# Output weights of the second pair: the first cast, low part and first sum later in their attention period

## The chip, the core and the metric

The kernel runs on one core of a Trainium2 chip. The core has five engines with instruction queues of their own: TensorE (PE, matrix products), VectorE (DVE), ScalarE (ACT), GpSimd (POOL) and SyncE (SP, which here issues the transfers between the chip's memory, HBM, and the core's own memory). Each engine takes its instructions in the order in which they stand; a wait at the head of a queue holds up everything behind it. The metric is the device time of one execution in microseconds (us).

## The reference

The kernel computes one encoder block on 512 tokens of width 2048 in float32:

```
h  = RMSNorm(x)
[qa|ka|va|qb|kb|vb|f] = h @ W_in
oa = stick-breaking attention (8 heads)      ob = forgetting attention (8 heads)
x  = x + concat(headnorm(oa), headnorm(ob)) @ W_out
x  = x + relu(RMSNorm(x) @ W_up)^2 @ W_down
y  = RMSNorm(x)
```

The change concerns `W_out`, 2048 x 2048, while the attention runs: its rows are prepared there for the product that comes behind the attention.

## The kernel before, in words

Every float32 product is made of three products of parts. An operand is split into a high part, a copy rounded to float32r (ACT, "cast"), and a low part, the difference (DVE, "low"); `mm3` (L76 to L79) multiplies high by high, low by high and high by low.

The attention stage handles 16 heads in 17 periods of a written timetable, `TPER` = 26.05 units each. In period n, PE projects the query and the key of head n, forms the scores of head n - 1 and the value product and the norm's sums of head n - 2, all in turn. The projections use four weight pieces per period (`Piece`, load L163 on SP into `wraw`, cast L170 on ACT into `wh`, low part L177 on DVE into `wl`), two for the query and two for the key.

For a head of the forgetting kind, DVE adds the biases to the scores (L840), GpSimd masks them (L779), DVE takes row maxima (L847, L848), ACT the exponentials (L852), and DVE divides by the row sums (L855, L857). ACT then sets the 16-bit halves apart (L872), SP transposes them in a transfer (L876), ACT joins them again (L880) and splits them (L884, with L887 on DVE). After the value product (tile `o`), ACT squares it, copies it and casts the square (L928, L929, L930); DVE makes the square's low part (L933); PE sums over the partitions with two matmuls (L938, L939, tile `ssq`); ACT and DVE finish the norm (L942, L943, L948 to L951). The query's result is scaled (L739), cast (L743, tile `uh`) and its low part made (L747, tile `ul`): these are "the query's parts". The key's are made by the same lines, with L737 ahead, at the beginning of the next period.

Beside this the output weights are prepared, in pairs of rows by `WeightSums`. For the pairs m = 0 to 3 (`whole`) a pair takes two periods, of which the first starts at `e` and the second at `o` = `e` + `TPER`. Two transfers (L968) bring four blocks into the tile `mixed`, which is free until the heads' results go there. The first cast (L972, `high`) and low part (L975, `low`) go to the tile `tboth`, which is stored to `wraws` (L976); four sums (L980, `sum`), a sixth cast and low part (L984, L988) follow, and stores (L989, L992).

The order of all this is a table: `plan.at(t, f)` enters a step at a time t, `plan.run` sorts by t and issues the steps so. The times are no waits; they only set the order on PE, ACT and DVE. The loads and stores on SP follow the table too up to entry 55.05; behind it a scheduler places them by its own estimates, between what they depend on. For m = 1, `e` is the start of period 2 in the table (52.1).

Of the kernel before, what the change touches and what calls it, by code (L numbers as in the profile page):

```python
# [37 lines left out]
def block_kernel(ctx, tc, x, g_attn, w_in, b_f, g_out_sb, g_out_fox, w_out, g_mlp, w_up, w_down, g_final, y):  # L38
# [104 lines left out]
    def v_columns(h):  # L143
        return 2 * WSB + h * P if h < NH else o0 + 2 * WSB + (h - NH) * P
# [74 lines left out]
    with ExitStack() as stage:  # L219
# [70 lines left out]
        c0, m = v_columns(order[0]), 2 * P + NH  # L290
# [422 lines left out]
    with tc.tile_pool(name="att", bufs=1, side="right", reuse_waits="tile") as at, \  # L713
# [281 lines left out]
        def whole(m, t):  # L995
            w = WeightSums(m, (0, 1), lambda: mixed[:, :NH].rearrange("p (q a) n -> p q (a n)", a=2))
            e, o = (t, t + TPER) if m else (TPER, TPER)
            loads = (0.5 if m == 1 else -15.0, 2.7) if m else (20.5, 20.6)
            highs, lows_, sums_, sixth = ((e + 3.3, o + 3.3), (e + 4.5, o + 4.5), (e + 6.4, e + 16.3, o + 6.4, o + 16.3), (o + 10.7, o + 20.6)) if m > 1 else \
                ((e + 10.7, o + 3.3), (e + 11.15, o + 4.5), (e + 16.3, e + 24.9, o + 6.4, o + 16.3), (o + 10.7, o + 20.6)) if m else \  # L1000
                ((e + 4.0, e + 10.0), (e + 5.2, e + 11.0), (e + 6.4, e + 19.2, e + 20.6, e + 21.8), (e + 22.0, e + 24.0))
            for i in range(2):
                plan.at(t + loads[i], w.load, (i,))
                plan.at(highs[i], w.high, i)
                plan.at(lows_[i], w.low, i)
            for i in range(4):
                plan.at(sums_[i], w.sum, i)
            plan.at(sums_[1] + 0.1, lambda: w.store(0, 2))
            plan.at(sixth[0], w.high_6)
            plan.at(sixth[1], w.low_6)  # L1010
            plan.at(sixth[1] + 0.1, lambda: w.store(2, 4))
# [132 lines left out]
        for m in range(4):  # L1144
            whole(m, TPER * 2 * m)
# [764 lines left out]
    def down_at(k):  # L1910
        g, db, i, p, u0 = down[k]
        return g, db, i, p, u0, min(2, GROUPS[g][1] - u0)

    with tc.manual_schedule(engines={pe.engine, act.engine, dve.engine}):
        for k in range(-4, len(down)):
            g, db, i, p, u0, m = down_at(max(k, 0))
# [198 lines left out]
```

## Time and profile before

| | us |
|---|---|
| median of 3 runs | 2012.35 |
| their range | 2009.54 to 2012.75 |
| the profiled execution | 2012.1 |
| its span in the profile | 2010.4 |
| busy PE, DVE, ACT in the span | 1997.9, 1738.8, 1202.2 |

The profile shows one execution. Rows of a timeline give the start, the duration, the engine, the line in the kernel, the operation, the tile written and the tiles read, and in brackets how long the engine was idle before it and what ended this. In a row of matmuls, which overlap, the duration is longer than the step from one start to the next. Rows of the waits give the total, the count and the longest. Rows of windows give, for each stretch, its length, the busy time and count of PE, of PE's weight loads, DVE, ACT and POOL, the clock granted to PE (1.00 is full), the busy share of the transfer engines and GB/s. The attention stage lies at about 150 to 620 us of the span; the periods' boundaries are not marked in the trace, but the scores' matmuls (tile `s`) and the norm's sums (tile `ssq`) show which one it is. What stands at about 200 to 226 us is period 2, with query and key of head 2, softmax of head 1 and norm of head 0.

### The profile page before, as it was taken

How to read it: one execution, taken by the hardware profiler on the slowest of the kernel's cores; microseconds unless marked ns; L12 is line 12 of the kernel's file. 1: busy time of each engine (PE TensorE's matmuls, PEld its weight loads, DVE VectorE, ACT ScalarE, POOL GpSimd, SP SyncE). 2: the span in 40 equal slices, each digit the busy share in tenths (PEclk: the TensorE clock that was granted, in tenths of full speed). 3: DMA queues.
4: the chain of work that ended last, by engine and by line, in shares of the span. 5: the costliest groups of instructions: out<-in, count | busy, mean ns of one | idle time of the engine just before them, and what ended most of it. 6: DMA issues, size and time to landing. Idle time of an engine off the chain costs nothing.

```text
span 2010.4 us, 27058 instructions
## 1 busy us (share of the span) xinstructions
PE 1997.9 (99%) x10302; PEld 1730.5 (86%) x10302; DVE 1738.8 (86%) x1968; ACT 1202.2 (60%) x1645; POOL 58.3 (3%) x73
## 2 busy tenths in 40 slices
PE   9999999999999999999999999999999999999998
PEld 9998788888898889888888888888888888888887
DVE  7886777788878578999999999998798888988896
ACT  7544666777765565777676766767543444444344
POOL 0000000011110000000000000000000000000003
PEclk9999999999999999999999999999999999999999
DMA  7417877777668872566666676666794674674642
GB/s 253 161 68 247 269 241 215 212 212 217 207 218 279 292 255 95 172 208 209 207 190 211 194 222 189 210 199 235 252 327 172 232 273 153 234 264 170 216 161 86
DMA packets 309426, 423.54 MB, mean 211 GB/s; under 512 B 49408, under 2 KB 205104, under 8 KB 302768
## 3 DMA queue, kind: packets, MB, share of 16 engines
q1 hardware_dynamic: 308544, 419.71, 63.8%
q10 hardware_dynamic: 752, 2.11, 0.3%
q8 instruction: 81, 1.33, 0.3%
q14 instruction: 49, 0.40, 0.1%
HBM read 315.45 MB, written 96.49 MB: 205 GB/s over the span
## 4 chain that ended last, share of the span: by engine, by line
PE 96%; DVE 1%; DMA 1%; ACT 0%; SPq 0%; issue 0%; ACTq 0%; DVEq 0%
PE psa L1287 11%; PE accd L78 8%; PE accd L79 8%; PE accd L77 8%; PE psa L1285 6%; PE psc L1287 5%; PE accq L77 5%; PE accq L79 5%; PE accq L78 5%; PE psc L1285 3%; PE psb L1287 3%; PE psb L1285 1%; PE m L78 1%; PE m L77 1%; PE m L79 1%; PE accoa L79 1%
## 5 line engine op out<-in xcount | busy, mean ns | idle before, releaser
L1923 ACT CAST wh<-wd 128x1024 fp32r<-128x1024 f32 x126 | 124.9, 999 | 168.7 <-PE accd L79 61.0
L1809 DVE TENSOR_TENSOR wl<-wu,wh 128x1024 fp32r<-128x1024 f32 x158 | 192.8, 1220 | 12.1 <-ACT wh L1803 11.9
L77 PE MATMUL accq<-hH,wh 128*128 128x512 f32 x512 | 200.8, 392 | 0.0
L79 PE MATMUL accq<-hH,wl 128*128 128x512 f32 x512 | 200.1, 391 | 0.0
L78 PE MATMUL accq<-hL,wh 128*128 128x512 f32 x512 | 199.8, 390 | 0.0
L1803 ACT CAST wh<-wu 128x1024 fp32r<-128x1024 f32 x158 | 167.5, 1060 | 43.8 <-issue 26.7
L1287 PE MATMUL psa<-f,wh 128*128 128x512 f32 x720 | 179.0, 391 | 0.0
L78 PE MATMUL accd<-wl,uf 128*128 128x512 f32 x436 | 169.6, 389 | 0.0
L79 PE MATMUL accd<-wh,uf 128*128 128x512 f32 x436 | 169.6, 389 | 0.0
L77 PE MATMUL accd<-wh,uf 128*128 128x512 f32 x436 | 169.4, 389 | 0.0
L1287 PEld LDWEIGHTS psa<-f,wh 128*128 128x128 f32 x720 | 132.3, 188 | 25.6
L1930 DVE TENSOR_TENSOR wl<-wd,wh 128x1024 fp32r<-128x1024 f32 x126 | 144.1, 1152 | 10.6 <-ACT wh L1923 10.6
L1923 ACT CAST wx<-wd 128x1024 fp32r<-128x1024 f32 (+1 forms) x82 | 80.8, 994 | 106.9 <-PE accd L79 43.4
L1644 DVE TENSOR_TENSOR m<-m,accd 128x1024 f32<-128x1024 f32 x84 | 102.3, 1218 | 47.1 <-PE accd L79 47.1
L79 PEld LDWEIGHTS accq<-hH,wl 128*128 128x128 f32 x512 | 96.4, 188 | 20.4
L78 PEld LDWEIGHTS accq<-hL,wh 128*128 128x128 f32 x512 | 96.6, 189 | 19.3
L77 PEld LDWEIGHTS accq<-hH,wh 128*128 128x128 f32 x512 | 96.6, 189 | 19.0
L77 PE MATMUL accd<-wx,uf 128*128 128x512 f32 x284 | 110.5, 389 | 0.0
L78 PE MATMUL accd<-wx,uf 128*128 128x512 f32 x284 | 110.5, 389 | 0.0
L79 PE MATMUL accd<-wx,uf 128*128 128x512 f32 x284 | 110.5, 389 | 0.0
L1285 PEld LDWEIGHTS psa<-f,wl 128*128 128x128 f32 x720 | 96.0, 191 | 5.4
L1285 PE MATMUL psa<-f,wl 128*128 128x256 f32 x720 | 98.3, 282 | 0.0
(443 smaller groups left out, 5118.1 us busy)
## 6 DMA issues: line engine op xcount, KB each, us to landing
wu<-in_w_up_dram SPq DMA_DIRECT2D x60, 1024.0 KB, 6.5
ufd<-st SPq DMA_DIRECT2D x98, 512.0 KB, 3.9
wd<-in_w_down_dram SPq DMA_DIRECT2D x48, 1024.0 KB, 8.5
uf<-ufd SPq DMA_DIRECT2D x42, 1024.0 KB, 7.5
wraw<-in_w_in_dram SPq DMA_DIRECT2D x68, 512.0 KB, 6.0
wo<-wsums SPq DMA_DIRECT2D x28, 512.0 KB, 4.4
q<-in_w_in_dram SPq DMA_DIRECT2D x32, 384.0 KB, 5.6
wd<-in_w_down_dram SPq DMA_DIRECT2D x16, 768.0 KB, 5.4
```

Of the source, the lines that this page charges most:

```text
L77: pe.matmul(out, sh, mh, start=first, stop=False, skip_group_check=True)
L78: pe.matmul(out, sh, ml, start=False, stop=False, skip_group_check=True)
L79: return pe.matmul(out, sl, mh, start=False, stop=last, skip_group_check=True)
L1285: ins = pe.matmul(ps[:, 2 * P:], lo[:, a, :], f_parts(p, a)[0], start=False, stop=last, skip_group_check=True)
L1287: ins = pe.matmul(ps, hi[:, a, :], f_both(p, a), start=a == PAIRS[0] and p in (1, 5), stop=last, skip_group_check=True)
L1644: dve.tensor_tensor(M[p][:, :, db, :], M[p][:, :, db, :], ps, op=ALU.add)
L1803: act.copy(rooms[k][0], srcs[k])
L1809: lows[0] = dve.tensor_tensor(lo, srcs.pop(k), hi.bitcast(F32), op=ALU.subtract)
L1923: act.copy(rooms[k + 3][0], srcs[k + 3])
L1930: dve.tensor_tensor(rooms[k + 2][1], srcs.pop(k + 2), rooms[k + 2][0].bitcast(F32), op=ALU.subtract)
```

## The change

The table's entries of the pair m = 1 change in three places; the middle branch of the three is that of m = 1.

```
             highs, lows_, sums_, sixth = ((e + 3.3, o + 3.3), ...) if m > 1 else \
-                ((e + 10.7, o + 3.3), (e + 11.15, o + 4.5), (e + 16.3, e + 24.9, o + 6.4, o + 16.3), (o + 10.7, o + 20.6)) if m else \
+                ((e + 19.0, o + 3.3), (e + 20.55, o + 4.5), (e + 20.6, e + 24.9, o + 6.4, o + 16.3), (o + 10.7, o + 20.6)) if m else \
```

The first cast moves from `e` + 10.7 to `e` + 19.0, the first low part from `e` + 11.15 to `e` + 20.55, the first sum from `e` + 16.3 to `e` + 20.6. PE's and GpSimd's orders stay as they are; the number of instructions does too.

On ACT, in period 2, these rows stood before, from the cast of the third weight piece on (`tboth` holds the high and low part of the output weights, `pl` here is the square's high part):

```order
L170 CAST wh<-wraw 128x1024
L972 CAST tboth<-mixed 128x512
L170 CAST wh<-wraw 128x1024
L852 ACTIVATE w,ml<-w,ml 128x128
L852 ACTIVATE w,ml<-w,ml 128x256
L852 ACTIVATE w,ml<-w,ml 128x384
L852 ACTIVATE w,ml<-w,ml 128x512
L928 ACTIVATE ph<-o 128x512
L929 COPY os<-o 128x512
L930 CAST pl<-ph 128x512
L743 CAST uh<-qf 128x512
L942 ACTIVATE ra<-ssq,eps 128x512
```

And these stand there now:

```order
L170 CAST wh<-wraw 128x1024 x2
L852 ACTIVATE w,ml<-w,ml 128x128
L852 ACTIVATE w,ml<-w,ml 128x256
L852 ACTIVATE w,ml<-w,ml 128x384
L852 ACTIVATE w,ml<-w,ml 128x512
L928 ACTIVATE ph<-o 128x512
L929 COPY os<-o 128x512
L930 CAST pl<-ph 128x512
L743 CAST uh<-qf 128x512
L972 CAST tboth<-mixed 128x512
L942 ACTIVATE ra<-ssq,eps 128x512
```

The cast L972 left the place between the third and the fourth piece's casts and stands behind the query's cast L743, ahead of the norm's L942.

On DVE, at the same place of the program, before (L887 is the low part of head 0's transposed weights, the L177 rows are the third and the fourth piece's low parts):

```order
L887 TENSOR_TENSOR pl<-pt,ph 128x1280
L975 TENSOR_TENSOR tboth<-mixed,tboth 128x512
L177 TENSOR_TENSOR wl<-wraw,wh 128x1024
L847 TENSOR_REDUCE ml<-w 128x1 x4
L848 TENSOR_SCALAR ml<-ml 128x4
L739 SCALAR_TENSOR_TENSOR qf<-accq,rb 128x512
L177 TENSOR_TENSOR wl<-wraw,wh 128x1024
L980 TENSOR_TENSOR mixed<-mixed 128x1024
L855 RECIPROCAL ml<-ml 128x4
```

And now, from the fourth piece's low part on; ahead of it the rows are the same without L975:

```order
L177 TENSOR_TENSOR wl<-wraw,wh 128x1024
L855 RECIPROCAL ml<-ml 128x4
L857 TENSOR_SCALAR w<-w,ml 128x128
L857 TENSOR_SCALAR w<-w,ml 128x256
L857 TENSOR_SCALAR w<-w,ml 128x384
L857 TENSOR_SCALAR w<-w,ml 128x512
L933 TENSOR_TENSOR pl<-ph,pl 128x512
L747 TENSOR_TENSOR ul<-qf,uh 128x512
L975 TENSOR_TENSOR tboth<-mixed,tboth 128x512
L980 TENSOR_TENSOR mixed<-mixed 128x1024
L948 SCALAR_TENSOR_TENSOR ph<-ssq,ra 128x512
```

L975 and L980 left their places ahead of the row maxima and ahead of the reciprocal; both stand behind the query's low part L747 and ahead of the norm's L948.

On SP, the store of `tboth` (L976) and the load of the next period's first weight piece (L163) change places:

```order
 L968 DMA mixed<-in_w_out_dram 128x2048
-L976 DMA wraws_93<-tboth 128x2x512
-L163 DMA wraw<-in_w_in_dram 128x8x128
+L163 DMA wraw<-in_w_in_dram 128x8x128
+L976 DMA wraws_93<-tboth 128x2x512
 L876 DMA_TRANSPOSE pl<-pt 128x20x128
```

The store now stands directly ahead of the transposing transfer of head 1.

## The prediction

> **What bounds the kernel now.** I read the page's busy times first, then the waits of TensorE, then the clock around the longest wait, and last the engines' timelines there.
>
> ```profile
> PE 1997.9 (99%) x10302; PEld 1730.5 (86%) x10302; DVE 1738.8 (86%) x1968; ACT 1202.2 (60%) x1645; POOL 58.3 (3%) x73
> ```
> ```profile
> PE ssq L938 <- ACT pl L930: 2.5, 1, 2.5
> PE vx L303 <- DVE still L299: 1.6, 1, 1.6
> PE ssq L939 <- DVE pl L933: 0.5, 1, 0.5
> ```
>
> TensorE (PE) is busy for 99% of the span, so only time that PE loses counts. Its waits are few: one at the start (L303), and the two matmuls of one sum of squares, L938 and L939, which head 0's norm needs in period 2 (n = 2, about 200 to 226 us). All other periods have none. The same place is the only stretch inside the kernel's attention stage where the granted clock (PEclk, the column behind POOL) drops:
>
> ```profile
> 221.00:222.00 1.00, 0.14 (x1) 0.00 (x0) 1.00 (x2) 1.00 (x5) 0.00 (x0) 1.00 0.99 389
> 224.00:225.00 1.00, 0.50 (x2) 0.41 (x2) 1.00 (x2) 0.06 (x1) 0.00 (x0) 0.82 0.19 58
> 225.00:226.00 1.00, 1.00 (x3) 0.74 (x3) 0.14 (x1) 0.59 (x1) 0.00 (x0) 0.50 0.00 0
> 228.00:229.00 1.00, 1.00 (x5) 0.81 (x5) 0.93 (x3) 0.98 (x1) 0.00 (x0) 0.98 0.00 0
> ```
> ```profile
> 220.52 0.39 PE L78 MATMUL accq<-hL,wh 128*128 128x512 f32 x1
> 220.75 0.39 PE L79 MATMUL accq<-hH,wl 128*128 128x512 f32 x1
> 223.59 0.50 PE L938 MATMUL ssq<-pl,onesr 128*128 128x512 f32 x1 [2.45 <-ACT pl L930]
> 224.59 0.78 PE L939 MATMUL ssq<-pl,onesr 128*128 128x512 f32 x1 [0.50 <-DVE pl L933]
> 225.17 0.63 PE L77 MATMUL accq<-hH,wh 128*128 128x512 f32 x1
> 228.12 0.40 PE L78 MATMUL accq<-hL,wh 128*128 128x512 f32 x1
> ```
>
> In step with the matmuls ahead of it, which start every 0.23 us (220.52, 220.75), L938 would have started at 220.98. It starts at 223.59, L939 a whole microsecond later, and the eight matmuls up to 228.12 run at half clock for the most part. From 220.98 to 228.12 stand 10 steps (two of the sum, eight of the projection, the last beginning at 228.12): at full rate 9 x 0.23 = 2.07 us for the nine that precede it, against 7.14 us. This place costs 5.1 us, and that is the most that the change can win here.
>
> Who is late is seen on ScalarE (ACT) and VectorE (DVE):
>
> ```profile
> 215.42 0.62 ACT L972 CAST tboth<-mixed 128x512 fp32r<-128x512 f32 x1 [3.42 <-DMA mixed<-in_w_out_dram]
> 216.94 1.05 ACT L170 CAST wh<-wraw 128x1024 fp32r<-128x1024 f32 x1 [0.90 <-DMA wraw<-in_w_in_dram]
> 219.77 0.40 ACT L852 ACTIVATE w<-w,ml 128x128 f32<-128x128 f32 x1 [1.78 <-DVE ml L848]
> 222.91 0.62 ACT L930 CAST pl<-ph 128x512 fp32r<-128x512 f32 x1
> 223.43 0.62 ACT L743 CAST uh<-qf 128x512 fp32r<-128x512 f32 x1
> 225.41 0.69 ACT L942 ACTIVATE ra<-ssq,eps 128x512 f32<-128x512 f32 x1 [1.36 <-PE ssq L939]
> 226.67 2.31 ACT L872 COPY pt<-w 128x2560 uint16<-128x2560 uint16 x1
> ```
> ```profile
> 211.09 1.49 DVE L887 TENSOR_TENSOR pl<-pt,ph 128x1280 fp32r<-128x1280 f32 x1 [0.84 <-ACT ph L884]
> 216.07 0.69 DVE L975 TENSOR_TENSOR tboth<-mixed,tboth 128x512 fp32r<-128x512 f32 x1 [3.49 <-ACT tboth L972]
> 216.68 1.22 DVE L177 TENSOR_TENSOR wl<-wraw,wh 128x1024 fp32r<-128x1024 f32 x1
> 217.82 1.66 DVE L847 TENSOR_REDUCE ml<-w 128x1 f32<-128x128 f32 x4
> 219.51 0.17 DVE L848 TENSOR_SCALAR ml<-ml 128x4 f32<-128x4 f32 x1
> 220.19 1.21 DVE L177 TENSOR_TENSOR wl<-wraw,wh 128x1024 fp32r<-128x1024 f32 x1
> 221.32 1.22 DVE L980 TENSOR_TENSOR mixed<-mixed 128x1024 f32<-128x1024 f32 x1
> 222.66 1.27 DVE L857 TENSOR_SCALAR w<-w,ml 128x128 f32<-128x128 f32 x4
> 223.85 0.69 DVE L933 TENSOR_TENSOR pl<-ph,pl 128x512 fp32r<-128x512 f32 x1
> ```
> ```profile
> 206.40 8.94 DMA mixed<-in_w_out_dram
> ```
>
> The load of the output weights' first half (mixed) lands at 215.34. ACT's cast L972 waits 3.42 us for it, DVE's L975 waits 3.49 us for the cast. Behind L975 stand, in order, a weight piece's low part (L177), head 1's row maxima (L847, L848), and only then may ACT begin the exponentials (L852). Behind these stand L928, L929 and L930, for which L938 waits. So a load that nobody needs here soon holds up the chain L975, L177, L847, L848, L852, L930, L938.
>
> **The change, part by part.** Three compute instructions move, nothing is added: the cast (0.62 us, row 215.42), the low part (0.69, row 216.07) and the sum (1.22, row 221.32), and with the low part its store (wraws), which falls behind a load on SP's queue.
>
> *ACT without L972.* The next instruction is L170, the cast of the period's fourth piece. It waited for its own load until 216.94, after L972 had left, and that load does not hang on the moved work; it is issued ahead of it on SP:
>
> ```profile
> 206.95 4.94 SPq L163 DMA_DIRECT2D wraw<-in_w_in_dram  x2
> 216.79 0.38 SPq L976 DMA_DIRECT2D wraws<-tboth  x1
> 217.93 0.49 SPq L163 DMA_DIRECT2D wraw<-in_w_in_dram  x1
> 229.00 2.52 SPq L876 DMA_TRANSPOSE pl<-pt  x1
> ```
>
> The row at 206.95 merges two piece loads, the second of which is the fourth piece's. I keep 216.94: ACT is then free at 217.99 (1.05 us). Its next start overlaps the end by 0.10, as row 222.91 with its 0.62 us and row 223.43 show.
>
> *DVE without L975.* L887 ends at 212.58, so L177 can run from 212.5 to 213.7, the four maxima (1.66) to 215.4 and L848 to 215.5. That is before ACT is free. So L852 starts at 217.89, where the cast lets it, and not at 219.77: 1.88 us earlier. L930 keeps its distance, ends at 221.65 (before 222.91 + 0.62 = 223.53), and L938 starts at 221.71. PE's wait falls from 2.45 to about 0.6 us.
>
> *DVE without L980.* L933, for which L939 waits, stood behind L177, L980 and L857. L177 of the fourth piece now follows its cast (218.05 to 219.27); the reciprocal needs the last exponential (about 220.2), L857 ends near 221.7, and L933 runs from 221.70 to 222.39. L939 starts at 222.44, 2.15 us earlier than 224.59. The gap that L980 leaves is filled by the wait for ACT, so of its 1.22 us only what lies in these 2.15 is won.
>
> *The clock.* The gap in PE shrinks from 2.45 + 0.50 us to about 0.6 + 0.4. No row shows what a gap of one microsecond does to the clock. Bounds: the slow stretch stays as it is (gain 2.15 alone), or goes. If it goes, the projection's first matmul starts 0.35 us behind L939 (0.58 at half clock in the rows 224.59 and 225.17, less 0.23 by which a full-rate step is shorter), and seven more at 0.23 bring the matmul of 228.12 to 224.40: gain 3.72 us. I take this: by the windows' means the half clock lasted from about 224.64 (0.82 is 0.36 us at half) to 228.04 (0.98), if the two microseconds between are like 225 to 226. These 3.4 us stand just behind 3.4 us in which PE did almost nothing but L938, while in the new order it idles for 1.0 us of them and works for over two thirds.
>
> [...]
>
> *Where the moved work now stands.* On ACT L972 comes behind L743 and ahead of L942, which waits for L939. L743 ends at about 222.2, L972 at 222.7, L942 cannot start before 223.1: hidden by that wait (ACT stood idle 1.36 us at row 225.41). On DVE L975 and L980 run from 222.9 to 224.7, where L948 waits for L943 until about 224.4: some 0.3 us later than it could be, and off PE's path. On SP the store is issued at about 223.7; the transposing load (row 229.00), which waits for L872 to end at about 226.7, is behind it. The queue's one other passed item, the next piece's load of 217.93, waits for the L177 that ended at 217.90 and now ends at 213.7; it can only go out earlier.
>
> *Is the gain kept?* PE is 3.72 us ahead in period 3, while the store and the transposes are only about 2.1 us ahead. In that period head 1's sum has these rows:
>
> ```profile
> 242.79 0.62 ACT L984 CAST thi<-mixed 128x512 fp32r<-128x512 f32 x1 [1.54 <-DMA wraws<-tboth]
> 249.23 0.62 ACT L930 CAST pl<-ph 128x512 fp32r<-128x512 f32 x1
> ```
> ```profile
> 250.17 0.68 DVE L933 TENSOR_TENSOR pl<-ph,pl 128x512 fp32r<-128x512 f32 x1
> ```
> ```profile
> 252.21 0.39 PE L938 MATMUL ssq<-pl,onesr 128*128 128x512 f32 x1
> 252.44 0.39 PE L939 MATMUL ssq<-pl,onesr 128*128 128x512 f32 x1
> ```
>
> L930 ends 2.36 us and L933 1.6 us before PE takes them. The difference of 3.72 - 2.15 = 1.6 us between PE's lead and the transfers' lead uses up this slack and does not pass it. I cost it at nothing, with L984's wait for the second store (1.54 us now) as what is late next.
>
> Sum: the profiled execution took 2012.1 us, 1.7 more than its span; 2012.1 - 3.72 = 2008.4 us. The median shown, 2012.35, is 0.25 above this execution, so against it the gain is 0.20%, and 0.2% (4.0 us, about what a measurement of this kernel can tell from no change) lies at 2008.33.
>
> **The rivals.**
>
> One, *the stall goes whole*: if the fourth piece lands 0.6 us earlier than 216.94, L938 is in step and PE wins the 5.1 us: 2007.0. For it speaks that this landing ends a backlog of transfers and that the runs lie 3.2 us apart (2009.54 to 2012.75); against it, that nothing in the change speeds that load.
>
> Two, *the gap shrinks and the slow clock stays* (the slow stretch has another cause than this gap), or the fourth piece lands late: 2012.1 - 2.15 = 2010.0. Each microsecond by which the piece lands past 216.94 takes one off the gain, and past 218.8 nothing of the earlier L852 is left. Against it: PE's idle time falls to a third.
>
> Three, *slower*: period 3's store of the second tboth decides. L984 waits for its landing already, and L763, L170, L852 and L930 stand behind it on ACT. It lands at 242.79 now. If transfers are the limit there it moves up 2.1 us, to 240.7, and L933 ends just in time. From there on PE waits a microsecond for each. With the slow clock that a wait of 2.45 us brings (1.6 us, the difference of 3.72 and 2.15) the gain is gone at a landing of 242.8, and one at 246.8 gives about 2012.1 - 3.7 + 6.1 + 1.6 = 2016.1. For it: transfers are dense in this stage. Against it: the moved store goes out where the transfers stand idle (PE rows 225 to 229 have DMA share 0.00), so less is queued, not more.
>
> A fourth, small: part of this happens and the new wait gives back some 2 us: 2010.5.
>
> **How the numbers follow.** The sum's own case gets 0.54, with its own range 2007.3 to 2009.5 (0.5 us either way for the piece's landing, 0.3 for the steps between, and the 0.25 between profiled and median run); half of it lies below 2008.33. Rival one gets 0.22, rival two 0.11, the fourth 0.06, rival three 0.07. Faster by over 0.2%: 0.22 + 0.27 = 0.49; slower: 0.07; the rest, 0.44, within 0.2%. The range 2006.8 to 2010.8 holds the sum's case, most of rival one and two and part of the fourth, and leaves out rival three and the tails.
>
> **What would show it.** In the changed profile L972 stands behind L743 with no wait ahead of it. L170 ahead of L852 still waits for its load, now for nearly 5 us, and ends near 218. L938 waits about 0.6 us for L930, L939 a few tenths for L933, and PEclk is 1.00 from 221 to 229. L948 follows L980 without a gap. In period 3 no PE wait appears. The prediction is wrong if PEclk still drops, if the fourth piece lands at another time, or if PE's list of waits has a new row after 230 us.

## The result, and the profile after

The changed kernel takes 2007.91 us (median of 16 runs, 2006.98 to 2011.13), the kernel before 2011.77 (16 runs, 2008.33 to 2012.99). The ratio is 0.9983, with an interval of 0.9976 to 0.9990. So 3.9 us are gained, 0.17%, clear of the measurement's noise and just within the 0.2% named in the prediction. The profiled execution took 2007.39 us. Of all executions reported below, one, of the kernel with ten extra matmuls, took 2848.28 us at a mean clock of 0.654; it is a slow one and is left out of every count and median here.

TensorE's waits and the granted clock (the third figure from the end in each row of the windows) after the change:

```profile
PE vx L303 <- DVE still L299: 1.6, 1, 1.6
PE ssq L938 <- ACT pl L930: 0.3, 1, 0.3
PE accoa L79 <- DVE g L60: 0.3, 1, 0.3
PE ssq L939 <- DVE pl L933: 0.2, 1, 0.2
```
```profile
224.00:225.00 1.00, 1.00 (x6) 0.84 (x5) 0.97 (x2) 1.00 (x1) 0.00 (x0) 1.00 0.91 350
225.00:226.00 1.00, 1.00 (x6) 0.81 (x5) 0.93 (x3) 0.60 (x1) 0.00 (x0) 1.00 0.00 0
```

The waits for L930 and L933 fell from 2.45 and 0.50 us to 0.31 and 0.23, and the clock stays at 1.00. The order of the queues is the one forecast, seen in the timelines of ACT, DVE and SP:

```profile
216.00 1.05 ACT L170 CAST wh<-wraw 128x1024 fp32r<-128x1024 f32 x1 [4.88 <-DMA wraw<-in_w_in_dram]
216.96 0.39 ACT L852 ACTIVATE w<-w,ml 128x128 f32<-128x128 f32 x1
220.09 0.62 ACT L930 CAST pl<-ph 128x512 fp32r<-128x512 f32 x1
221.13 0.62 ACT L972 CAST tboth<-mixed 128x512 fp32r<-128x512 f32 x1
222.03 0.69 ACT L942 ACTIVATE ra<-ssq,eps 128x512 f32<-128x512 f32 x1 [0.28 <-PE ssq L939]
```
```profile
212.75 1.66 DVE L847 TENSOR_REDUCE ml<-w 128x1 f32<-128x128 f32 x4
220.75 0.69 DVE L933 TENSOR_TENSOR pl<-ph,pl 128x512 fp32r<-128x512 f32 x1
221.96 0.69 DVE L975 TENSOR_TENSOR tboth<-mixed,tboth 128x512 fp32r<-128x512 f32 x1
222.68 1.22 DVE L980 TENSOR_TENSOR mixed<-mixed 128x1024 f32<-128x1024 f32 x1
223.82 0.68 DVE L948 SCALAR_TENSOR_TENSOR ph<-ssq,ra 128x512 f32<-128x512 f32 x1
```
```profile
214.98 0.38 SPq L163 DMA_DIRECT2D wraw<-in_w_in_dram  x1
222.67 0.38 SPq L976 DMA_DIRECT2D wraws<-tboth  x1
225.62 2.52 SPq L876 DMA_TRANSPOSE pl<-pt  x1
```

The maxima (L847) run at 212.75 instead of 217.82. ACT now waits 4.88 us for a weight piece's load, and the exponentials (L852) follow it without a gap. L972, L975 and L980 stand where nothing of the chain is behind them, and L948 follows L980 at once. On PE the place reads:

```profile
220.07 0.39 PE L79 MATMUL accq<-hH,wl 128*128 128x512 f32 x1
220.77 0.49 PE L938 MATMUL ssq<-pl,onesr 128*128 128x512 f32 x1 [0.31 <-ACT pl L930]
221.49 0.50 PE L939 MATMUL ssq<-pl,onesr 128*128 128x512 f32 x1 [0.23 <-DVE pl L933]
221.83 0.39 PE L77 MATMUL accq<-hH,wh 128*128 128x512 f32 x1
223.44 0.39 PE L78 MATMUL accq<-hL,wh 128*128 128x512 f32 x1
```

In step, L938 would have started at 220.30; the eighth matmul of the projection starts at 223.44. That is 3.14 us for what took 7.14 before, 4.0 us less. Of these, 2.4 lie ahead of L939 (1.19 us from the step to L939's start, 3.61 before) and 1.6 behind it (1.95 against 3.53): wait and clock. The two profiled spans differ by 4.7 us (2010.4 and 2005.7). The other 0.7 us were there before the place: the last matmul ahead of L938 starts at 220.07 here and at 220.75 there, and the transfer L755, ahead of every instruction that moved, is issued at 195.03 here and at 195.75 there. They belong to the two executions, not to the change.

### The profile page after: what moved, and what is told of

The parts are those of the page before. It is cut to its first block, busy times and chain, and to the rows that moved or that the text cites. A ratio compares the mean times of both kernels' runs of the same rounds, so it can differ in the third digit from the quotient of the medians.

```text
span 2005.7 us, 27059 instructions
## 1 busy us (share of the span) xinstructions
PE 1995.6 (99%) x10302; PEld 1729.5 (86%) x10302; DVE 1738.9 (87%) x1968; ACT 1202.1 (60%) x1645; POOL 58.0 (3%) x73
## 4 chain that ended last, share of the span: by engine, by line
PE 97%; DMA 1%; DVE 1%; ACT 0%; issue 0%; SPq 0%; ACTq 0%; DVEq 0%
PE psa L1287 11%; PE accd L78 8%; PE accd L79 8%; PE accd L77 8%; PE psa L1285 6%; PE psc L1287 5%; PE accq L77 5%; PE accq L79 5%; PE accq L78 5%; PE psc L1285 3%; PE psb L1287 3%; PE psb L1285 1%; PE m L77 1%; PE m L79 1%; PE m L78 1%; PE accoa L79 1%
```

## The experiments

The theory: the low part L975 stood at the head of DVE's queue, waiting by way of L972 for a load, and held up the maxima and so the exponentials, the norm's cast and PE; PE's idle time then made the clock fall. The rivals: the sum on DVE or the cast on ACT did it; the weight piece's load did it; the clock's fall has another cause.

**The sum alone.** Cast and low part stay.

```
-                (..., (e + 16.3, e + 24.9, o + 6.4, o + 16.3), ...) if m else \
+                (..., (e + 20.6, e + 24.9, o + 6.4, o + 16.3), ...) if m else \
```

> The kernel before, with the first sum alone moved behind the query's parts (entry e + 20.6 instead of e + 16.3); cast and low part stay. Theory (the low part ahead of the row maxima is what holds up ACT, and with it PE): ACT is as late as before, L938 still waits about 2.4 us, only L939 comes some 0.25 us earlier; the time is that of before less 0.3 us, PEclk drops as before. Rival (the sum between the last low part and the division is a real part of the stall): L939 comes over 1 us earlier and 1 to 2.5 us are gained.

Measured: 2011.06 us, ratio 1.0000 (0.9991 to 1.0009). PE's timeline:

```profile
222.86 0.65 PE L938 MATMUL ssq<-pl,onesr 128*128 128x512 f32 x1 [2.41 <-ACT pl L930]
223.58 0.79 PE L939 MATMUL ssq<-pl,onesr 128*128 128x512 f32 x1
```

L938 waits as before; L939 follows 0.72 us behind it instead of 1.00. This is what the theory expected of the sum: some 0.3 us, too small to be measured as time. The rival falls.

**The weight piece alone.** In the kernel before, the cast and low part of the piece whose load ACT waits for at 216.94 go behind the norm's.

```
-                        if a == 0 and n == NH + 1:
-                            cast, low = -12.35, -10.95
+                        if a == 0 and n in (3, NH + 1):
+                            cast, low = (-8.9, -6.8) if n == 3 else (-12.35, -10.95)
```

> The kernel before, with only that piece's cast and low part moved, and the output weights' steps where they were. Theory (before, the low part of the output weights held the chain, the piece's load came in its shadow): L852 starts where it did, the time is that of before less 0 to 0.4 us, PEclk drops. Rival (the piece's load alone is the holder): the gain of the changed kernel or more, 4 to 5 us.

Measured: 2011.24 us, ratio 1.0000 (0.9991 to 1.0009). ACT, PE and the clock, which falls as before:

```profile
214.87 0.62 ACT L972 CAST tboth<-mixed 128x512 fp32r<-128x512 f32 x1 [3.10 <-DMA mixed<-in_w_out_dram]
219.22 0.40 ACT L852 ACTIVATE w<-w,ml 128x128 f32<-128x128 f32 x1 [3.73 <-DVE ml L848]
```
```profile
223.04 0.50 PE L938 MATMUL ssq<-pl,onesr 128*128 128x512 f32 x1 [1.98 <-ACT pl L930]
```
```profile
226.00:227.00 1.00, 1.00 (x4) 0.81 (x3) 0.97 (x2) 1.00 (x1) 0.00 (x0) 0.50 0.00 0
```

The exponentials now wait for nothing but the maxima (3.73 us for L848), and PE waits 1.98 us. With the low part at its old place the piece's load is not what holds them.

**The low part alone.** Only the order on DVE changes (and on SP that of the store behind the low part); ACT's order is that of before, so the cast still waits ahead of the exponentials.

```
-                ((e + 10.7, o + 3.3), (e + 11.15, o + 4.5), ...
+                ((e + 13.0, o + 3.3), (e + 14.45, o + 4.5), ...
```

> The kernel before, with the low part alone moved on DVE from ahead of the row maxima to just behind them and the query's scaling; the cast on ACT and the sum stay where they were. Theory (a wait at the head of DVE's queue ahead of the maxima is all of it): the whole gain of the changed kernel, less about 0.15 us for the sum ahead of the division: 3.5 to 3.9 us, ratio 0.9982, and PEclk stays at 1.00. Rival (the cast's wait on ACT is what holds up the exponentials): no gain.

Measured: 2007.59 us, ratio 0.9985 (0.9976 to 0.9994). DVE, then ACT, then PE's waits:

```profile
212.72 1.66 DVE L847 TENSOR_REDUCE ml<-w 128x1 f32<-128x128 f32 x4
215.13 0.69 DVE L975 TENSOR_TENSOR tboth<-mixed,tboth 128x512 fp32r<-128x512 f32 x1
```
```profile
214.47 0.62 ACT L972 CAST tboth<-mixed 128x512 fp32r<-128x512 f32 x1 [3.38 <-DMA mixed<-in_w_out_dram]
215.99 1.05 ACT L170 CAST wh<-wraw 128x1024 fp32r<-128x1024 f32 x1 [0.89 <-DMA wraw<-in_w_in_dram]
216.94 0.40 ACT L852 ACTIVATE w<-w,ml 128x128 f32<-128x128 f32 x1
```
```profile
PE ssq L938 <- ACT pl L930: 0.4, 1, 0.4
```

The whole gain is there. L972 still waits 3.38 us on ACT, and that costs nothing, because the piece's load holds ACT beyond it anyway (L170 waits another 0.89 us). What counted was one place in DVE's queue: a waiting step of 0.69 us ahead of the maxima.

**What is left.** In the changed kernel, that piece's cast and low part go behind the norm's as well (the edit of the second experiment, on the changed kernel).

> The changed kernel, and in addition the cast and low part of the first weight piece of period 3 (the one whose load ACT waits for ahead of the exponentials) moved behind head 0's norm cast and low part in period 2. Theory (what is left of the wait is that piece's load, which nobody needs in this period): L938 and L939 wait for nothing, 1.1 us less than the changed kernel, about 5.0 us less than before, ratio 0.9975. Rival (what is left is the length of the chain from the maxima on): the same as the changed kernel, ratio 0.998. A later cast could also make the piece late in period 3: then a new wait at its start and less gain than the changed kernel.

Measured: 2006.61 us (2005.76 to 2007.79), ratio 0.9980 (0.9971 to 0.9989). PE and ACT:

```profile
219.21 0.39 PE L79 MATMUL accq<-hH,wl 128*128 128x512 f32 x1
219.44 0.39 PE L938 MATMUL ssq<-pl,onesr 128*128 128x512 f32 x1
219.66 0.39 PE L939 MATMUL ssq<-pl,onesr 128*128 128x512 f32 x1
```
```profile
213.69 0.40 ACT L852 ACTIVATE w<-w,ml 128x128 f32<-128x128 f32 x1 [3.59 <-DVE ml L848]
217.35 1.05 ACT L170 CAST wh<-wraw 128x1024 fp32r<-128x1024 f32 x1
```

L938 and L939 run in step. The exponentials follow the maxima; the piece's cast, 217.35, has its load long there. Against the kernel before of the same chip 4.9 us are gained. The changed kernel was not run beside it; its median of 2007.91 lies 1.3 us above, near the 1.1 expected. The intervals of the two ratios overlap, so it is the rows of PE, not the time alone, that show this last microsecond. This version is the fastest of all that ran, and no wait of PE is left in its attention stage: the later cast makes nothing late.

**The wait without the idle time.** In the kernel before, ten more matmuls on PE ahead of L938:

```
-        plan.at(0.2, load_rb)
+        plan.at(0.2, load_rb), plan.at(TPER * 2 + 20.2, lambda: [pe.matmul(
+            heads[1].s[:, 2 * P:6 * P], onesr, hH[0], start=True, stop=True) for _ in range(10)])
```

> The kernel before, with ten matmuls of 512 columns put on PE just ahead of head 0's norm sums in period 2; they write a part of the scores' tile that has been read already, and nobody reads what they write. They fill about 2.3 us of PE's wait and are extra work that the reference does not have. Theory (PE's idle time causes the slow clock): L938 starts where it did, but PEclk stays at 1.00, and 1.6 us are gained against before. Rival (the slow clock has another cause than this gap): PEclk drops to 0.5 for 3.4 us as before, gain 0. If the ten matmuls stick out of the gap, some tenths are lost.

Measured: 2010.01 us (median of 11 runs), against 2011.70 of the kernel before on that chip; ratio 0.9994 (0.9985 to 1.0002). PE and the clock where it was 0.50 before:

```profile
220.18 2.43 PE L1143 MATMUL s<-hH,onesr 128*128 128x512 f32 x10
222.83 0.49 PE L938 MATMUL ssq<-pl,onesr 128*128 128x512 f32 x1 [0.23 <-ACT pl L930]
```
```profile
225.00:226.00 1.00, 1.00 (x6) 0.80 (x5) 0.25 (x1) 0.97 (x3) 0.00 (x0) 1.00 0.00 0
```

L938 is as late as ever, but the clock stays at full rate and by the medians 1.7 us are won by work that nobody needs. As a ratio this is not clear of the noise. The clock decides: a stretch of 3.4 us at half rate is 0.0008 of the span. The clock also falls behind the last matmul of the kernel; half rate from there to the end of the span is another 0.0006 (one copy more, below) to 0.0014 (changed, piece moved) in the four profiles of which the last section gives that fall. The seven profiled executions without the stretch at L938 read a mean clock of 0.999, the four with it 0.998; by these sums a short fall at the end could still hide the stretch in a reading of 0.999. It reads 0.999 in the 11 executions of this kernel, and 0.998 or less (0.997 in two) in 69 of the 83 of the kernel before that stood beside the experiments.

**The gap made longer again.** The changed kernel with ACT's copy L929 made several times for head 0; here two copies more:

```
-                act.copy(self.os, self.o)
+                [act.copy(self.os, self.o) for _ in range(3 if self.i == 0 else 1)]
```

> The changed kernel, with ACT's copy of head 0's output (L929) made three times instead of once, which holds up the norm's cast by 2 x 0.46 us. Theory (microsecond for microsecond, and the clock holds while the gap is well under 2.45 us): L938 waits about 1.2 us, PEclk stays at 1.00, 0.9 us slower than the changed kernel. Rival (the clock drops at any gap over a microsecond): 0.9 + 1.6 = 2.5 us slower than the changed kernel.

Measured: 2010.89 us (2007.77 to 2012.91), 3.0 above the changed kernel. Its profiled execution shows a wait of 1.28 us and the full clock:

```profile
221.05 0.50 PE L938 MATMUL ssq<-pl,onesr 128*128 128x512 f32 x1 [1.28 <-ACT pl L930]
```
```profile
223.00:224.00 1.00, 1.00 (x6) 0.79 (x6) 1.00 (x1) 0.97 (x3) 0.00 (x0) 1.00 0.13 51
```

but 7 of its 10 executions have a mean clock of 0.998. So both expectations missed: this version has the slow clock in some executions and not in others. The three without it, of which the profiled one is one, lie at 2007.8 to 2008.7, the seven with it at 2010.1 to 2012.9. How long PE waited in those seven is not known; it need not have been 1.28 us.

Four copies more:

> The changed kernel, with that copy made five times. Theory (the gap is again nearly that of before, 2.1 us, and brings the slow clock back): L938 waits about 2.1 us, PEclk drops to 0.5 for 3.4 us, 1.85 + 1.6 = 3.4 us slower than the changed kernel, nearly the time of before. Rival (no link of gap and clock, or the limit is higher than 2.1 us): PEclk stays at 1.00, 1.85 us slower than the changed kernel.

Measured: 2011.90 us, and 0.998 in 10 of 10 executions. The gap:

```profile
223.89 0.49 PE L938 MATMUL ssq<-pl,onesr 128*128 128x512 f32 x1 [3.69 <-ACT pl L930]
```
```profile
226.00:227.00 1.00, 1.00 (x3) 0.72 (x3) 1.00 (x2) 1.00 (x2) 0.00 (x0) 0.50 0.30 117
```

The slow clock is back, and so is the time of before. The size was wrong: the wait is 3.69 us, not 2.1. A repeated copy takes 0.62 us and not 0.46 (four more take 2.5), and the piece landed some 0.9 us later against PE than in the changed kernel's profile.

One copy more:

> The changed kernel, with ACT's copy of head 0's output (L929) made twice instead of once; the runs with three and five copies showed 0.62 us for each more, so L938 waits about 0.9 us. [...] Rival (a fixed length of gap decides, whatever its place): all executions or none.

Measured: 2008.04 us, 0.998 in 2 of 11 executions. The profiled one waits only 0.37 us, as the piece landed early in it (0.6 us earlier against PE than in the changed kernel's profile). The count is neither all nor none; it lies between the changed kernel's 1 of 16 and the 7 of 10, the median 0.1 above the changed kernel. Two of 11 and one of 16 cannot be told apart, so this run only says that the step from rare to frequent lies between one copy more and two.

The wait of before, half filled, with five matmuls in place of the ten:

> The kernel before, with five extra matmuls of 512 columns on PE just ahead of head 0's norm sums, which nobody reads; they fill 1.15 us of the wait and leave about 1.3 us of it, as much as three copies left in the changed kernel. [...] Rival (the clock's fall hangs on the late load, not on PE's idle time): 0.998 as often as before.

Measured: 2009.89 us against 2011.17 beside it, ratio 0.9995 (0.9986 to 1.0004), 0.998 in 2 of 11 executions. PE:

```profile
219.65 1.29 PE L1143 MATMUL s<-hH,onesr 128*128 128x512 f32 x5
221.66 0.49 PE L938 MATMUL ssq<-pl,onesr 128*128 128x512 f32 x1 [0.72 <-ACT pl L930]
```

With the late load untouched and the idle time cut to 0.72 and 0.51 us, the slow clock became rare. It hangs on PE's idle time, not on the load. All counts together, with medians that were not all measured side by side:

| kernel | waits of L938, L939 in its profile, us | mean clock 0.998 or less | median, us |
|---|---|---|---|
| changed, four copies more | 3.69, 0.23 | 10 of 10 | 2011.90 |
| before | 2.45, 0.50 | 69 of 83 | 2011.43 |
| before, sum moved | 2.41, none | 9 of 11 | 2011.06 |
| before, piece moved | 1.98, 0.22 | 11 of 11 | 2011.24 |
| changed, two copies more | 1.28, 0.23 | 7 of 10 | 2010.89 |
| before, five matmuls | 0.72, 0.51 | 2 of 11 | 2009.89 |
| before, low part moved | 0.43, 0.23 | 1 of 11 | 2007.59 |
| changed, one copy more | 0.37, 0.23 | 2 of 11 | 2008.04 |
| changed | 0.31, 0.23 | 1 of 16 | 2007.91 |
| before, ten matmuls | 0.23, 0.50 | 0 of 11 | 2010.01 |
| changed, piece moved | none, none | 0 of 11 | 2006.61 |

The waits are those of one execution each and vary with the loads (against PE the piece landed 0.9 us later with four copies more than in the changed kernel's profile, 0.6 us earlier with one), so the table is an order, not a law. In the row of two copies more, the waits are even those of an execution that kept the full clock.

## Why the prediction was right

**The place and its price.** Right. 7.14 us were to shrink by 3.72, they shrank by 4.00 in the profile. The time came out at 2007.91 for 2008.4; against the medians the gain was 3.9, as the sum's 3.95 from the median shown.

**ACT without L972, DVE without L975.** Right in kind. L852 was to come 1.88 us earlier; with the 0.68 us between the two executions taken off it came 2.13 earlier (219.77 - 0.68 - 216.96), since the piece landed 0.26 earlier (216.94 - 0.68 - 216.00). So L938's wait is 0.31 and not 0.6. The low part run alone showed that L975 was the holder and L972 was not.

A name was wrong, though not a number. The prediction and the part on the change call the load at 216.94 that of period 2's fourth piece. By the table's entries it is the first piece of period 3 (its cast stands at -12.35 of that period, behind the fourth piece's, which is the row of 210.95 in the kernel before); and with three buffers in turn the load that now passes the store on SP is that period's third, not its first. The mistake hid that this cast need not stand ahead of the exponentials at all, which is where the last microsecond lay.

**L980.** Right: L939 came 2.4 us earlier (2.15 foretold), and alone the sum brought 0.3.

**The clock.** Right in the value taken; the row of the changed profile shows 1.00 throughout. Idle time as the cause was argued then and is shown now by the ten matmuls. What the prediction missed is that it differs from execution to execution: the kernel before did not always have the slow stretch, and one execution of the changed kernel, that of 2011.13 us, has a mean clock of 0.998; where its clock fell is not known, since it was not the profiled one. The length of the idle time differs too: the clock fell behind waits of 1.98 and 0.22 us (piece moved) and, at the end of the kernel, 2.04 us behind the last matmul (changed, piece moved), and it held through waits of 1.28 and 0.23 us (two copies more). The last section sets out the times of the falls.

**Where the moved work stands.** Right: hidden on all three queues, L948 directly behind L980.

**Is the gain kept?** Right that it is, wrong in the slack. The prediction had the transfers gain 2.15 us only and the slack of period 3 used up. The rows of period 3 show otherwise:

```profile
238.53 0.62 ACT L984 CAST thi<-mixed 128x512 fp32r<-128x512 f32 x1 [1.71 <-DMA wraws<-tboth]
244.52 0.62 ACT L930 CAST pl<-ph 128x512 fp32r<-128x512 f32 x1
```
```profile
247.50 0.39 PE L938 MATMUL ssq<-pl,onesr 128*128 128x512 f32 x1
```

L984 comes 4.26 us earlier than before and PE's L938 4.71 (0.7 of each belongs to the two executions), and between the end of L930 and L938 lie 2.36 us, exactly as before. The second store and its landing move nearly as far as the engines: L984's wait for it grew by 0.17 us only (1.71 for 1.54), and that does not reach PE. Nothing of rival three is seen.

**The rivals.** The first, the whole stall gone, did not happen by chance of the landing, but it is what the version with the piece moved does (4.9 us for 5.1). Of the second's slow clock there is a mean of 0.998 in one execution of 16, not seen in a profile. The chance of 0.49 for more than 0.2% and 0.44 for less was near an even bet, and the measured 0.17% with its interval of 0.10 to 0.24% straddles that line too.

## What to carry to other kernels

Where the bounding engine waits, follow the chain on every queue to the first step that waits for something the chain does not need; here it was one 0.69 us step at the head of DVE's queue, and moving it alone gave the whole gain, while two other moves did nothing by themselves. Ask of each step left in the chain which period needs it: the next holder was a cast for the period after. A stall on TensorE can cost more than its own length, as the granted clock may fall behind it (here 1.6 to 1.7 us more). Here it fell at that place in the four profiles in which the two waits come to 2.20 us or more, and in none of the seven with 1.51 us or less. As the fall differs between executions, read the clock of many runs and not of one profile.

## What the runs showed that was not expected

The clock does not fall at a fixed time behind the wait. In the profiles it falls at two places: behind L938 in four of them, and behind the last matmul of the kernel, for which four profiles stand below. The means of the windows give the times of the falls behind L938, to within 0.01 us (0.59 in the 0.2 us from 224.60 before; 0.53, 0.72 and 0.53 in the microseconds from 223, 224 and 225 in the three others; the next window reads 0.50 in each):

| profile | waits of L938, L939, us | L938 starts | clock falls there | from start to fall, us |
|---|---|---|---|---|
| before | 2.45, 0.50 | 223.59 | 224.64 | 1.05 |
| before, sum moved | 2.41, none | 222.86 | 223.06 | 0.20 |
| before, piece moved | 1.98, 0.22 | 223.04 | 224.44 | 1.40 |
| changed, four copies more | 3.69, 0.23 | 223.89 | 225.06 | 1.17 |

The stretch at half clock lasts 3.4 us in all four. At the end, where TensorE has nothing more to do, the fall comes 2.04 us behind the last matmul's end in the changed kernel with the piece moved, 3.60 us in the changed kernel (1997.98 to 2001.58), 3.69 us in the kernel before (2002.70 to 2006.39) and 5.27 us with one copy more. These are the two extremes (changed with the piece moved, then changed with one copy more):

```profile
1996.16 0.28 PE L79 MATMUL acce<-ws,us 128*128 128x256 f32 x1
1998.00:1999.00 1.00, 0.00 (x0) 0.00 (x0) 0.93 (x4) 0.52 (x1) 0.00 (x0) 0.74 0.00 0
```
```profile
1997.37 0.28 PE L79 MATMUL acce<-ws,us 128*128 128x256 f32 x1
2002.00:2003.00 1.00, 0.00 (x0) 0.00 (x0) 0.00 (x0) 0.00 (x0) 0.00 (x0) 0.96 1.04 399
```

A fixed length of idle time does not fit these rows: the clock held for 5.27 us without a matmul in one profile and fell behind 1.98 and 0.22 us in another. What sets the moment of the fall is not shown by any run. At L938 the two waits come to 2.20 us or more in the four profiles in which the clock fell, and to 1.51 us or less in the seven in which it did not.

The profiled execution of the version with two copies more, with 1.28 and 0.23 us, kept the full clock. The seven executions of that version at 0.998 took 3.4 us longer on average than the three others, and the slow stretch accounts for 1.6 to 1.7 of that; from these numbers I estimate that they waited some 1.7 us longer. In the kernel before, likewise, the executions at 0.998 or less lie at 2010.1 to 2014.8 us and those at 0.999 at 2008.2 to 2009.9, and their means differ by 2.8 us (2011.77 and 2008.98). Longer waits in the executions with the slow stretch would account for the rest, but no run recorded the waits of executions that were not profiled, so this stays open.

Useless matmuls in a wait kept the clock up: with ten of them the median went from 2011.70 to 2010.01 us without changing when the waiting matmul starts. As a time this is not clear of the noise (the ratio's interval ends at 1.0002); the mean clock, 0.999 in 11 of 11 executions, is.
